# One row of a late load is split off by columns and dealt out by partitions 0 to 125 and 126 to 127

## The chip, the cores and the metric

The kernel runs on one core of one Trainium2 chip. The metric is device time in microseconds (us), and lower is better. Times of whole runs come as a median of several runs; the profile is one profiled execution of the same program.

## The reference

```python
def setup_inputs():
    batch, seq, dim = 32, 512, 1024
    return {"x": np.random.randn(batch, seq, dim).astype(np.float32)}

def reference(x):
    relu_x = np.maximum(x, 0)
    return np.sum(relu_x, axis=-1).astype(np.float32)
```

The input has 32 x 512 = 16,384 rows of 1,024 float32 numbers, 67.1 MB. Of each row the negative numbers are set to zero and the rest is summed, so the output is 16,384 numbers, 64 KB.

## The kernel before

The 16,384 rows lie on 128 partitions, so each partition has 128 rows, and these come as 8 blocks of 16 rows. A block is 64 KB per partition and 8.4 MB in all. Three buffers (`io`) in the on-chip memory take the blocks in turn. All loads and stores are issued by SP (SyncE) on one queue and share the core's 16 DMA engines. The order of the work is written out by hand: every load has a semaphore of its own, and a load that reuses a buffer waits on the count `sems.dve` that says that VectorE (DVE) has done with it.

- **Blocks 0 to 6** (the loop over `NB` in `relu_sum`): ScalarE (ACT) clamps the block in place in pieces (`clamp`, L145), VectorE sums each piece (`total`, L153). Of block 6 ACT takes two rows with sum (`act_row`, L160) and block 6's last eight rows go to VectorE, which clamps and sums a row in one instruction (`dve_row`, L168, 14 such rows up to the end).
- **The last 16 rows** come in smaller loads, so that the work behind the last byte is short. `TAIL = [8, 4]` gives a load of 8 rows and a load of 4 rows per partition; in each, rows are shared between ACT and VectorE one by one. The last four rows come as four loads that are cut by columns of the partition's 4,096 numbers: 2,302 columns, then the last 873 columns, then 518, and at the very end 403 columns into a tile named `last`. ACT, VectorE and GpSimd (POOL, L246) clamp and sum the parts (`act_part` L122, `dve_part` L127); one instruction of VectorE (L266) joins the parts of the last row but one.
- **The stores** (`store`, L115 and L116): the sums of block 0, the sums of nearly all other rows, and at the very end the sums of the last two rows.

TensorE multiplies a few tiles from the buffers beside the tail (L186); nothing reads its result.

The load of 4 rows per partition is one DMA of 128 partitions x 4,096 numbers (16,384 bytes per partition, 2 MB). Its first row is ACT's and its second VectorE's, each of which waits for 16 counts on the load's semaphore; then ACT and VectorE take one more row each. "The twelfth of the last 16 rows" is the last row of this load. Behind it in the queue stand the loads of 2,302, 873, 518 and 403 columns.

Of the kernel before, what the change touches and what calls it, by code (L numbers as in the profile page):

```python
# [10 lines left out]
NBUF = 3  # L11
# [15 lines left out]

EARLY = 1
N_MM, MM_COLS = 8, 512


def kernel(tc: tile.TileContext, x: bass.AP, out: bass.AP):
    nc = tc.nc
    sems = Semaphores(tc)

    tc.close()
    tc.compile()
    nc.cur_bb = nc.bb_map[tc.start_bb_name]
    body = nc.cur_bb.bb.instructions
    ends = list(body)  # L40
    body.clear()
    n_stores = relu_sum(nc, sems, x, out)
    body.extend(ends)


    nc.cur_bb = nc.bb_map[tc.start_bb_name + "_end"]
    nc.cur_bb.bb.instructions.clear()
    nums = sorted(s.num for s in (*sems.loads, sems.act, sems.dve))
    cleared = range(nums[0], nums[-1] + 1)
    assert len(cleared) == len(nums)  # L50
    nc.sync.sem_clear(cleared)
    nc.sync.wait_ge(sems.stored, 16 * n_stores).then_inc(sems.stored, -16 * n_stores)
    open_without_barrier(tc, EARLY)
# [12 lines left out]
def relu_sum(nc, sems: Semaphores, x: bass.AP, out: bass.AP):  # L66
    x_flat = x.flatten_outer_dims()
    N, D = x_flat.shape
    NT = N // P
    NB = len(TWO)  # L70
# [5 lines left out]
    res = nc.alloc_sbuf_tensor("res", [P, NT], F32)  # L76
# [13 lines left out]
    def rows(m, n):  # L90
        if m < ROWS:
            return xf[:, m : m + n, :]
        return xv[:, m - ROWS : m - ROWS + n, :]
# [6 lines left out]
    n_load = n_act = n_dve = n_store = 0  # L100

    def load(dst, src, after=None):
        nonlocal n_load
        dma = nc.sync.dma_start(out=dst, in_=src)  # L104
        if after:
            dma.wait_op(sems.dve, after[1], "sem-ge")
        dma.then_inc(sems.loads[n_load], 16)
        n_load += 1
        return sems.loads[n_load - 1]

# [44 lines left out]
        ).wait_op(sems.act, n_act, "sem-ge").then_inc(sems.dve, 1)  # L155
        n_dve += 1

    def act_row(ap, accum_out, loaded):
        nonlocal n_act
        i = nc.scalar.activation(out=ap, in_=ap, func=RELU, accum_out=accum_out)  # L160
        if loaded is not None:
            i.wait_op(loaded, 16, "sem-ge")
        i.then_inc(sems.act, 1)
        n_act += 1

    def dve_row(ap, accum_out, loaded):
        nonlocal n_dve
        i = nc.vector.tensor_scalar(  # L168
            out=ap,
            in0=ap,  # L170
            scalar1=0.0,
            scalar2=None,
            op0=MAX,
            op1=ADD,
            accum_out=accum_out,
        )
        if loaded is not None:
            i.wait_op(loaded, 16, "sem-ge")
        i.then_inc(sems.dve, 1)
        n_dve += 1  # L180

# [10 lines left out]
    freed = []  # L192
    m = 0
    for j in range(NB):
        buf = bufs[j % NBUF]
        loaded = load(buf[:, :, :], rows(m, ROWS), j >= NBUF and freed[j - NBUF])
        c = 0
        act_waits = dve_waits = loaded
        for n in TWO[j]:
            clamp(buf[:, c : c + n, :], act_waits)  # L200
            total(buf[:, c : c + n, :], m + c, n)
            act_waits = None
            c += n
        for _ in range(ACT[j]):
            act_row(buf[:, c, :], res[:, m + c : m + c + 1], act_waits)
            act_waits = None
            c += 1
        for _ in range(DVE[j]):
            dve_row(buf[:, c, :], res[:, m + c : m + c + 1], dve_waits)
            dve_waits = None  # L210
            c += 1
        assert c == ROWS
        freed.append((n_act, n_dve))
        m += ROWS
# [2 lines left out]
    multiply(freed[-1][1])  # L217
    buf = bufs[NB % NBUF]
    c = 0
    for n in TAIL:  # L220
        loaded = load(
            buf[:, c : c + n, :], rows(m, n), None if c else freed[NB - NBUF]
        )
        for i in range(n):
            if i % 2 == 0 or (n == 8 and i == 7):
                act_row(buf[:, c, :], res[:, m : m + 1], loaded if i == 0 else None)
            else:
                dve_row(buf[:, c, :], res[:, m : m + 1], loaded if i == 1 else None)
            c += 1
            m += 1  # L230

    flat = buf[:, :, :].rearrange("p c d -> p (c d)")
    src = rows(m, 4).rearrange("p c d -> p (c d)")
    at = c * D
    head = 2 * D + HEAD
# [2 lines left out]


    loaded = load(flat[:, at : at + head], src[:, :head])  # L240
    act_row(buf[:, c, :], res[:, m : m + 1], loaded)
    sums_act = n_act
    dve_row(buf[:, c + 1, :], res[:, m + 1 : m + 2], loaded)
    sums_dve = n_dve
    clamped = flat[:, at + 2 * D : at + head]
    nc.gpsimd.tensor_scalar(  # L246
        out=clamped, in0=clamped, scalar1=0.0, scalar2=None, op0=MAX
    ).wait_op(loaded, 16, "sem-ge").then_inc(sems.end, 1)
    for lo, hi, n, first, second in (
# [3 lines left out]
        loaded = load(flat[:, at + lo : at + hi], src[:, lo:hi])  # L253
        act_part(flat[:, at + lo : at + lo + n], last[:, first : first + 1], (loaded, 16))
        dve_part(flat[:, at + lo + n : at + hi], last[:, second : second + 1], (loaded, 16))
    loaded = load(last[:, 2 : 2 + n_last], src[:, middle:end])
# [10 lines left out]
        out=clamped,  # L267
# [5 lines left out]
        accum_out=res[:, NT - 2 : NT - 1],  # L273
# [53 lines left out]
```

## Time and profile before

| | us |
|---|---|
| three runs | 160.9, 161.08, 161.12 |
| median of the runs | 161.08 |
| span of the profiled execution | 159.9 |
| between span and median of the runs | 1.18 |
| the 16 DMA engines' packets, share of the span | 97.8% |
| VectorE busy | 118.7 (74%) |
| ScalarE busy | 103.6 (65%) |
| last load has landed, start of the last sum (L266) | 158.05 |

The span runs from the first issue on SP to the landing of the last store, and is the profiled execution's own time; the time of a run has 1.0 to 1.2 us more around it. All DMA packets of the input, 67.1 MB, are in one queue. The 16 DMA engines can be told apart by the order of their packets: each load gives each engine eight packets, one for each of its eight partitions' rows, and then one increment of the load's semaphore; the work that waits for a load starts at the sixteenth increment.

### The profile page before, as it was taken

The numbers are of one execution on the slowest core, as the hardware profiler recorded it, in microseconds if no ns is written. First come the engines' busy times: TensorE is split into PE (matmuls) and PEld (weight loads), VectorE is DVE, ScalarE is ACT, GpSimd is POOL, SyncE is SP. The second block draws the span as 40 slices with busy tenths as digits, with TensorE's granted clock in tenths as the row PEclk, the third lists the DMA queues.
The fourth block names the chain that finished last, engine by engine and source line by source line (L and its number), as shares of the span: only waits on it lengthen the run. The fifth ranks groups of instructions, "written<-read, shape, count | busy, mean of one in ns | idle before, by whom it ended". The sixth has DMA issues, their size and how long they took to land.

```text
span 159.9 us, 157 instructions
## 1 busy us (share of the span) xinstructions
PE 8.6 (5%) x16; PEld 3.6 (2%) x16; DVE 118.7 (74%) x44; ACT 103.6 (65%) x53; POOL 1.0 (1%) x5
## 2 busy tenths in 40 slices
PE   0000000000000000000000000000000000000695
PEld 0000000000000000000000000000000000000241
DVE  0000000006999799999999999999999799999986
ACT  0000049993599807997099950999429993397995
POOL 0000000000000000000000000000000000000001
DMA  8996996996996997999979979969969969899993
GB/s 279 508 492 295 524 492 295 524 492 295 525 492 295 524 475 311 524 393 393 525 328 459 508 344 459 508 295 508 492 295 524 492 295 524 377 402 402 428 396 110
DMA packets 2304, 67.18 MB, mean 420 GB/s; under 512 B 640, under 2 KB 768, under 8 KB 1024
## 3 DMA queue, kind: packets, MB, share of 16 engines
q1 hardware_dynamic: 2304, 67.18, 97.8%
HBM read 67.11 MB, written 0.07 MB: 420 GB/s over the span
## 4 chain that ended last, share of the span: by engine, by line
DMA 45%; DVE 45%; ACT 9%; SPq 1%; issue 0%
DMA io<-in_x_dram 45%; DVE res L153 43%; ACT io L145 9%; DVE io L168 1%; SPq L104 1%; DVE io L127 1%; DVE io L266 0%
## 5 line engine op out<-in xcount | busy, mean ns | idle before, releaser
L153 DVE TENSOR_REDUCE res<-io 128x8 f32<-128x8192 f32 (+2 forms) x10 | 101.1, 10173 | 39.2 <-ACT io L145 39.2
L145 ACT ACTIVATE io<-io 128x8192 f32<-128x8192 f32 (+2 forms) x10 | 81.8, 8218 | 25.9 <-DMA io<-in_x_dram 25.9
L160 ACT ACTIVATE io<-io 128x1024 f32<-128x1024 f32 x18 | 18.8, 1042 | 6.6 <-DMA io<-in_x_dram 6.6
L186 PE MATMUL ps<-io 128*128 128x512 f32 x16 | 8.6, 698 | 149.5 <-DVE io L168 149.5
L168 DVE TENSOR_SCALAR_CACHE_REDUCE io<-io 128x1024 f32<-128x1024 f32 x14 | 16.2, 1215 | 0.5 <-DMA io<-in_x_dram 0.4
L143 ACT ACT_TABLE_LOAD x1 | 1.3, 1283 | 22.3 <-DMA io<-in_x_dram 22.3
L186 PEld LDWEIGHTS ps<-io 128*128 128x128 f32 x16 | 3.6, 231 | 153.7 <-DVE io L168 149.5
L160 ACT ACTIVATION_READ_ACCUMULATOR io<-io 128x1 f32 x18 | 3.3, 186 | 0.0
L246 POOL TENSOR_SCALAR io<-io 128x254 f32<-128x254 f32 x1 | 0.8, 841 | 155.4 <-DMA io<-in_x_dram 155.4
L168 DVE DVE_READ_ACCUMULATOR io<-io 128x1 f32 x14 | 1.2, 82 | 0.0
L127 DVE TENSOR_SCALAR_CACHE_REDUCE io<-io 128x552 f32<-128x552 f32 (+1 forms) x2 | 1.1, 594 | 0.0
L122 ACT ACTIVATE io<-io 128x321 f32<-128x321 f32 (+1 forms) x2 | 0.9, 426 | 0.1
L266 DVE SCALAR_TENSOR_TENSOR io<-last,io 128x254 f32<-128x254 f32 x1 | 0.4, 423 | 0.0
L122 ACT ACTIVATION_READ_ACCUMULATOR io<-io 128x1 f32 x2 | 0.4, 186 | 0.0
L122 ACT ACTIVATE last<-last 128x153 f32<-128x153 f32 x1 | 0.3, 330 | 0.0
L122 ACT ACTIVATION_READ_ACCUMULATOR last<-last 128x1 f32 x1 | 0.2, 187 | 0.0
L127 DVE DVE_READ_ACCUMULATOR io<-io 128x1 f32 x2 | 0.2, 82 | 0.0
L311 POOL MEMSET const-uint8-127<- 128x1 uint8 x1 | 0.1, 102 | 0.0
L311 POOL MEMSET const-bfloat16-1.0<- 128x1 bf16 x1 | 0.1, 101 | 0.0
L311 POOL MEMSET const-float32-0.0<- 128x1 f32 x1 | 0.1, 99 | 0.2 <-issue 0.2
L311 POOL MEMSET const-float32-1.0<- 128x1 f32 x1 | 0.1, 98 | 0.0
L266 DVE DVE_READ_ACCUMULATOR io<-last,io 128x1 f32 x1 | 0.1, 82 | 0.0
## 6 DMA issues: line engine op xcount, KB each, us to landing
io<-in_x_dram SPq DMA_DIRECT2D x1, 4096.0 KB, 23.7
io<-in_x_dram SPq DMA_DIRECT2D x1, 2048.0 KB, 28.3
io<-in_x_dram SPq DMA_DIRECT2D x1, 1151.0 KB, 30.6
io<-in_x_dram SPq DMA_DIRECT2D x1, 436.5 KB, 31.2
io<-in_x_dram SPq DMA_DIRECT2D x1, 259.0 KB, 31.4
last<-in_x_dram SPq DMA_DIRECT2D x1, 201.5 KB, 31.4
io<-in_x_dram SPq DMA_DIRECT2D x7, 29.0
out_dram<-res SPq DMA_DIRECT2D x1, 55.0 KB, 1.6
```

The costliest lines, as they stand in the source:

```text
L104: dma = nc.sync.dma_start(out=dst, in_=src)
L122: nc.scalar.activation(out=ap, in_=ap, func=RELU, accum_out=accum_out).wait_op(*after, "sem-ge").then_inc(sems.end, 1)
L127: i = nc.vector.tensor_scalar(out=ap, in0=ap, scalar1=0.0, scalar2=None, op0=MAX, op1=ADD, accum_out=accum_out,)
L143: nc.scalar.preload_act_table(RELU).wait_op(loaded, 16, "sem-ge")
L145: i = nc.scalar.activation(out=ap, in_=ap, func=RELU)
L153: nc.vector.tensor_reduce(out=res[:, m : m + n], in_=ap, axis=mybir.AxisListType.X, op=ADD).wait_op(sems.act, n_act, "sem-ge").then_inc(se ...
L160: i = nc.scalar.activation(out=ap, in_=ap, func=RELU, accum_out=accum_out)
L168: i = nc.vector.tensor_scalar(out=ap, in0=ap, scalar1=0.0, scalar2=None, op0=MAX, op1=ADD, accum_out=accum_out,)
L186: i = nc.tensor.matmul(ps[:, :], rows_of[:, 0, :P], rows_of[:, 1, :MM_COLS], start=True, stop=True)
L246: nc.gpsimd.tensor_scalar(out=clamped, in0=clamped, scalar1=0.0, scalar2=None, op0=MAX).wait_op(loaded, 16, "sem-ge").then_inc(sems.end, 1)
L266: nc.vector.scalar_tensor_tensor(out=clamped, in0=last[:, : 2 + LAST_DVE], scalar=0.0, in1=clamped, op0=MAX, op1=ADD, accum_out=res[:, NT ...
L311: nc = _bacc.Bacc("TRN2", target_bir_lowering=False, num_devices=1)
```

## The change

Of the load of 4 rows per partition, the last 334 columns (of 4,096, so 1,336 bytes of the 16,384) are left out and come in two loads of their own right behind it: one for partitions 0 to 125, one for partitions 126 and 127. All three increase the same semaphore, and the two instructions that waited for 16 counts on it now wait for 48. SP issues two DMAs more; nothing else is moved. The functions `act_row` and `dve_row` get the count as an argument, 16 by default.

```diff
+MOST, SHARED = 126, 334
...
     def load(dst, src, after=None):
+        return load_parts([(dst, src)], after)
+
+    def load_parts(parts, after=None):
         nonlocal n_load
-        dma = nc.sync.dma_start(out=dst, in_=src)
-        if after:
-            dma.wait_op(sems.dve, after[1], "sem-ge")
-        dma.then_inc(sems.loads[n_load], 16)
+        for dst, src in parts:
+            dma = nc.sync.dma_start(out=dst, in_=src)
+            if after:
+                dma.wait_op(sems.dve, after[1], "sem-ge")
+            dma.then_inc(sems.loads[n_load], 16)
+            after = None
         n_load += 1
         return sems.loads[n_load - 1]
...
+    flat = buf[:, :, :].rearrange("p c d -> p (c d)")
     for n in TAIL:
-        loaded = load(
-            buf[:, c : c + n, :], rows(m, n), None if c else freed[NB - NBUF]
-        )
+        count = 16
+        if c == 0:
+            loaded = load(buf[:, c : c + n, :], rows(m, n), freed[NB - NBUF])
+        else:
+            count = 16 * 3
+            src = rows(m, n).rearrange("p c d -> p (c d)")
+            at, cut = c * D, n * D - SHARED
+            loaded = load_parts(
+                [
+                    (flat[:, at : at + cut], src[:, :cut]),
+                    (flat[:MOST, at + cut : at + n * D], src[:MOST, cut:]),
+                    (flat[MOST:, at + cut : at + n * D], src[MOST:, cut:]),
+                ]
+            )
         for i in range(n):
             if i % 2 == 0 or (n == 8 and i == 7):
-                act_row(buf[:, c, :], res[:, m : m + 1], loaded if i == 0 else None)
+                act_row(buf[:, c, :], res[:, m : m + 1], loaded if i == 0 else None, count)
             else:
-                dve_row(buf[:, c, :], res[:, m : m + 1], loaded if i == 1 else None)
+                dve_row(buf[:, c, :], res[:, m : m + 1], loaded if i == 1 else None, count)
```

## The prediction

> **What bounds the kernel now.** I read the shares of busy time first, then the DMA queue, then the chain of waits.
>
> ```profile
> PE 8.6 (5%) x16; PEld 3.6 (2%) x16; DVE 118.7 (74%) x44; ACT 103.6 (65%) x53; POOL 1.0 (1%) x5
> ...
> q1 hardware_dynamic: 2304, 67.18, 97.8%
> ```
>
> The reader is to see that the packets of the DMA queue take 97.8% of what 16 DMA engines have, while VectorE has a quarter of the span free. The chain in order of time says the same of the end:
>
> ```profile
> 125.15 30.57 DMA io<-in_x_dram
> 155.72 0.02 issue
> 155.75 1.23 DVE io L168 x2
> 156.97 1.05 DVE io L127 x4
> 158.03 0.02 issue
> 158.05 0.43 DVE io L266 x2
> ```
>
> A load issued at 125.15 us lands at 155.72 us, and that is no slow transfer: it stands in the queue behind the loads before it. From then on VectorE has 2.26 us of work in a row (up to 158.01), and the last load lands at 158.03. So two things end within 0.02 us of each other: the work behind the load of 2,302 columns, and the last load itself. To make the end earlier, both loads must land earlier.
>
> Which of the 16 DMA engines lands last? Stretches of 0.1 us near the end show it; the last two numbers of a row are the mean busy share of the 16 engines and GB/s.
>
> ```profile
> core 0: us, PE busy (x) PEld busy (x) DVE busy (x) ACT busy (x) POOL busy (x), PEclk, DMA share, GB/s
> 156.40:156.50 0.10, 0.10 (x1) 0.01 (x1) 0.10 (x1) 0.10 (x1) 0.10 (x1) 1.00 1.09 394
> ...
> 156.80:156.90 0.10, 0.10 (x2) 0.04 (x1) 0.10 (x3) 0.10 (x3) 0.00 (x0) 1.00 0.74 243
> ...
> 157.00:157.10 0.10, 0.10 (x2) 0.02 (x1) 0.10 (x1) 0.10 (x1) 0.00 (x0) 1.00 0.28 60
> ...
> 157.20:157.30 0.10, 0.10 (x2) 0.07 (x1) 0.10 (x1) 0.10 (x2) 0.00 (x0) 1.00 0.09 32
> ...
> 157.40:157.50 0.10, 0.10 (x1) 0.00 (x0) 0.10 (x1) 0.04 (x1) 0.00 (x0) 1.00 0.10 21
> ```
>
> All engines work until 156.5; from 157.1 to 157.5 the share is 0.1 to 0.2, about two engines of 16. The increments of the load semaphores tell the same, load by load (us, for 14 engines and then the two late ones): four rows 151.97 to 152.43, then 152.82 and 152.93; 2,302 columns up to 155.22, then 155.61 and 155.72; 403 columns up to 157.56, then 157.91 and 158.03. Two engines are late by 0.35 to 0.50 us each time. They are not slower: a 64 KB packet takes 2.42 us on every engine, 27.1 GB/s. They are late from the start: the first packets of the 16 engines begin from 1.01 to 1.84 us, the two that begin last (1.61 and 1.84) end their first packet at 4.98 and 4.85, the others by 4.50. Since every engine gets the same bytes and never runs dry, the lag stays to the end.
>
> **The change, part by part.**
>
> 1. *The price of a packet.* The medians of the packet records are 68 ns for 1,612 bytes and 611 ns for 16,384. The line through both is 8.7 ns and 36.8 ns per 1,000 bytes. It gives 562 ns for the new 15,048 bytes and 58 ns for 1,336. Packets start 3 to 4 ns before the former one's record ends, so 54 to 58 ns is the range; I take 58.
>
> 2. *The 334 columns leave the main load.* Each engine's eight packets shrink by 49 ns each: 8 x 49 = 0.39 us less, on every engine.
>
> 3. *The load of 126 partitions.* The trace has no load on fewer than 128 partitions, so its dealing has to be bounded. In the trace 128 rows go as 8 to each of 16 engines, always evenly. 126 rows go evenly to 14 engines, 9 each, and neither to 15 nor to 16. The ends are 16 engines (7 or 8 rows each, nothing gained) and one engine (126 x 58 = 7.3 us); I take 14, as nearest to the even dealing seen. The cost is 9 x 58 = 0.52 us on each of the 14 engines, and none on the two left out. The Trainium skill, "DMA: Bandwidth & Descriptors", section "Why a DMA increments its semaphore by 16 and not by 1", says that the count of engines is the largest up to 16 that divides the slowest dimension, and that the lowest-numbered engines are taken; by that 14 are used too, but nothing here shows it.
>
> 4. *Which two are left out.* If rows are dealt in order, the two without rows are those that are served last, and the two late engines are those whose first packet began last. I take these for the same.
>
> 5. *The load of partitions 126 and 127.* Two rows of 58 ns, one on each of two engines, or both on one: 0.06 to 0.12 us there. If the first engines get them, these are ahead of the late ones by about half a microsecond.
>
> 6. *Two more issues on SP.* Issues at L104 took 327 to 486 ns, median 407, so the four loads behind and the first store are issued 0.8 us later. Cover: the last load's issue moves from 126.65 to 127.5, and its first bytes are due near 157; SP then waited 29.3 us (L115). Without that cover the cost would be the 0.8 us. I put it at nothing.
>
> 7. *The wait for 48 counts* stands at two instructions that waited for this load anyway. Behind ACT's and VectorE's row queue all later rows of their engine, and the last store waits for them. Before, VectorE waited until 152.95; it was free at 152.87. It costs nothing if the parts land earlier.
>
> **The sum.** The two late engines: 0.39 us earlier. The other fourteen: 0.52 - 0.39 = 0.13 us later (0.10 to 0.19, the last for one with a tenth row). At the load of 2,302 columns the late ones come to 155.33 and the others to 155.35: earlier by 0.37. At the last load the late ones come to 157.64 and the others to 157.56 + 0.13 = 157.69: earlier by 0.34. The engines follow: ACT is free at 155.34 and VectorE at 155.2, and VectorE's 2.26 us from 155.38 on end at 157.64. So the end moves by **0.34 us** (0.28 to 0.38), the profiled span from 159.9 to 159.56. Around the span the median run has 1.18 us, which I leave alone: **160.74 us**, own range 160.70 to 160.80. A measurement of this kernel can tell about 0.2% (0.32 us) from no change; the forecast lies barely beyond it.
>
> **Rivals.**
>
> *The destination is shared, so nothing is gained (161.0 to 161.08).* A packet's rate of 27.2 GB/s may be the limit of where it writes rather than of the engine. Now each engine writes the same eight partitions in every load; nine rows in a load of 14 engines must fall on partitions that other engines fill. If the late engines' partitions take in 27.2 GB/s at most, the 8 x 49 ns taken from a late engine return as waiting for the helpers' rows: 0.39 - 0.39 = 0, and the end stays but for gaps of 9 ns per packet (some 10 packets, 0.1 us). For it: all 16 engines run at one rate. Against it: an engine's own limit would look the same. The Trainium skill, "SBUF — State Buffer", section "Door 1: The DMA port swizzle", says that 16 ports to the partitions bound DMA at 27.2 GB/s each, which is this rule and speaks against the change; the 27.1 GB/s of the 64 KB packets agrees with the figure, not with where the limit sits.
>
> *The helpers get stuck (161.26 to 161.78).* The same crossing, but with time lost: if each of the 9 rows takes twice 58 ns, the fourteen end 9 x 116 - 392 = 0.65 us later, 0.18 behind the old end; if engines also lose as much on their own rows, 0.70. It decides from 96 ns a row (9 x 96 - 392 = 471, today's lead), and passes 0.2% at 132. For it: the first packets took up to 3.38 us in place of 2.42, so packets can be held up. Against it: from then on hardly one was.
>
> *Fewer engines than 14 (over 161.1).* With eight engines or fewer, 16 rows x 58 - 392 = 0.54 us exceeds the lead of 0.47. With two engines: 63 x 58 - 392 - 471 = 2.8 us, 163.9.
>
> *The wrong engines are spared (161.0 to 161.2).* If one of the late two stays among the fourteen, it lands 0.13 us later; the end moves by +0.01 to +0.13 us.
>
> **How the numbers follow.** The forecast has 0.57: 0.47 beyond 0.2%, 0.10 below it, since its bounds cross that line. The shared destination has 0.16 (0.13 within 0.2%, 0.03 slower), the wrong engines 0.08 (within), stuck helpers 0.15 and fewer engines 0.04 (both slower). That makes 0.47 faster, 0.31 same, 0.22 slower. The range runs from 160.55 (the largest gain, 0.38 us, and 0.15 us of scatter like that of the three runs) to 161.3, the cheaper end of the stuck helpers; it leaves out some 0.15.
>
> **What would show it.** In the profile after: at the four-row load and behind it the sixteen increments lie closer together, without two that are 0.35 us late; the share of 0.1 to 0.2 before the last landing is gone or shorter. There are 126 packets of 1,336 bytes on 14 engines, of 54 to 60 ns; far longer ones speak for the crossing. The load of 2,302 columns lands near 155.35 and the last near 157.69. I am wrong if two engines are late by half a microsecond as before, or if the packets of 1,336 bytes, or those of the late engines beside them, are stretched.

## The result and the profile after

The changed kernel takes 161.46 us (median of 20 runs, 161.23 to 161.91) against 161.1 us before (20 runs, 160.88 to 161.33). The ratio is 1.0023, 95% interval 1.0017 to 1.003: 0.36 us slower, where 0.34 us faster was forecast. The profiled execution took 161.29 us and has a span of 160.0 us. That is only 0.1 us more than the span of the trace before: the trace after is of one of the faster executions, and in the trace before the last engine happened to lag the most (see the mis-sized term below). So the loss is read here from the steps inside the traces, and its size from the medians.

The page, engines and DMA queue:

```profile
PE 8.7 (5%) x16; PEld 3.6 (2%) x16; DVE 118.8 (74%) x44; ACT 103.5 (65%) x53; POOL 1.0 (1%) x5
...
q1 hardware_dynamic: 2448, 67.18, 98.1%
```

The same bytes come in 144 packets more (128 of them rows of 1,336 bytes, 16 of them increments), and the engines' packets fill 98.1% of the span in place of 97.8%. The end of the chain in order of time:

```profile
125.72 29.97 DMA io<-in_x_dram
155.69 0.02 issue
155.72 1.23 DVE io L174 x2
156.94 1.09 DVE io L133 x4
158.04 0.02 issue
158.06 0.43 DVE io L283 x2
```

It is the chain of before within 0.03 us: the load of 2,302 columns lands at 155.69 (155.35 was forecast), the last one at 157.99 (157.69). The stretches of 0.1 us near the end show that this is not because nothing happened. The last two numbers are again the busy share and GB/s.

```profile
core 0: us, PE busy (x) PEld busy (x) DVE busy (x) ACT busy (x) POOL busy (x), PEclk, DMA share, GB/s
156.40:156.50 0.10, 0.10 (x1) 0.00 (x0) 0.10 (x1) 0.10 (x1) 0.10 (x1) 1.00 1.13 435
...
156.80:156.90 0.10, 0.10 (x1) 0.00 (x0) 0.10 (x3) 0.10 (x2) 0.00 (x0) 1.00 1.13 421
...
157.00:157.10 0.10, 0.10 (x2) 0.07 (x1) 0.10 (x1) 0.10 (x1) 0.00 (x0) 1.00 1.18 435
...
157.20:157.30 0.10, 0.10 (x1) 0.02 (x1) 0.10 (x1) 0.10 (x2) 0.00 (x0) 1.00 0.85 218
...
157.40:157.50 0.10, 0.10 (x2) 0.00 (x0) 0.10 (x1) 0.00 (x0) 0.00 (x0) 1.00 0.26 46
```

From 157.0 to 157.3 nearly all engines work now, where the share before was 0.28 and then 0.09, about four engines and then one or two. The sixteen increments of the last load (each engine's signal that its part has landed) lie within 0.36 us (157.64 to 157.99) where they had 0.93 (157.10 to 158.03). So the engines were evened out, but the early ones were brought back by half a microsecond and the late ones not brought forward. Where it was lost, stretches of 2 us show. Before:

```profile
151.00:153.00 2.00, 2.00 (x4) 0.84 (x3) 1.92 (x5) 2.00 (x5) 0.00 (x0) 1.00 0.99 417
153.00:155.00 2.00, 2.00 (x6) 0.82 (x5) 2.00 (x3) 2.00 (x5) 0.00 (x0) 1.00 0.96 396
```

After:

```profile
151.00:153.00 2.00, 2.00 (x4) 0.87 (x3) 1.69 (x4) 2.00 (x5) 0.00 (x0) 1.00 0.96 311
153.00:155.00 2.00, 2.00 (x6) 0.88 (x5) 2.00 (x3) 2.00 (x5) 0.00 (x0) 1.00 0.99 411
```

Between 151 and 153 us, when the rows of 1,336 bytes go, the engines are about as busy as before (0.96, before 0.99) and move 311 GB/s in place of 417: their packets got longer. The packet records say which. Most rows of 1,336 bytes take the 58 ns of the forecast, but the later ones up to 100; the eight packets of 9,208 bytes behind them have a median of 353 ns, yet the first of them takes 476 to 556 on every engine and the second up to 528, where none took more than 355 before.

For the experiments I use two numbers of a trace besides the time: from the increments of the load of 8 rows to those of the last load, the mean of the sixteen engines and the step from last to last. Before: mean 10.00, last 9.99 us. After: 10.45 and 10.16. The engines lost 0.45 us on average in that stage.

### The profile page after: what moved, and what is told of

Its sections match the earlier page's. It is cut to its first block, busy times and chain, and to the rows that moved or that the text cites. A ratio compares the mean times of both kernels' runs of the same rounds, so it can differ in the third digit from the quotient of the medians.

```text
span 160.0 us, 159 instructions
## 1 busy us (share of the span) xinstructions
PE 8.7 (5%) x16; PEld 3.6 (2%) x16; DVE 118.8 (74%) x44; ACT 103.5 (65%) x53; POOL 1.0 (1%) x5
## 3 DMA queue, kind: packets, MB, share of 16 engines
q1 hardware_dynamic: 2448, 67.18, 98.1%
## 4 chain that ended last, share of the span: by engine, by line
DVE 45%; DMA 44%; ACT 9%; SPq 1%; issue 0%
DMA io<-in_x_dram 44%; DVE res L159 43%; ACT io L151 9%; SPq L109 1%; DVE io L174 1%; DVE io L133 1%; DVE io L283 0%
```

## The experiments

Theories: **crossing** (rows that land on partitions which another engine fills in every other load lose time), against **packets** (more and smaller packets, issues, increments), **source** (rows read from memory that another engine reads) and **uneven deal** (14 engines carry more). Ratios are to runs of the kernel before on the same chip, with the 95% interval; all were timed in five rounds. "Mean" and "last" are of the one profiled execution of each kernel, and such an execution can lie up to 0.39 us from its kernel's median (e6 162.26 against 161.87, e5 161.60 against 161.28, e7 161.38 against 161.68), so differences of a few hundredths there are not secured.

| kernel | ratio | mean, us | last, us |
|---|---|---|---|
| before | 1 | 10.00 | 9.99 |
| the change | 1.0023 (1.0017 to 1.003) | 10.45 | 10.16 |
| e1_plain128 | 1.0009 (1.0001 to 1.0018) | 10.08 | 10.08 |
| e2_112_16 | 1.0028 (1.0017 to 1.004) | 10.43 | 10.40 |
| e3_source | 1.0004 (0.9996 to 1.0013) | 10.08 | 10.08 |
| e4_half | 1.0011 (1.0003 to 1.002) | 10.34 | 10.18 |
| e5_last | 1.0018 (1.0009 to 1.0027) | 10.36 | 10.38 |
| e6_double | 1.0056 (1.0043 to 1.007) | 11.00 | 11.15 |
| e7_halves | 1.0039 (1.0026 to 1.0051) | 10.42 | 10.43 |
| e8_tiny | 1.0003 (0.9993 to 1.0013) | 10.04 | 10.05 |
| e9_not_late | 1.0029 (1.0018 to 1.004) | 10.51 | 10.36 |
| e10_late_only | 1.0001 (0.9992 to 1.001) | 9.93 | 10.02 |
| e11_none | 0.9974 (0.9965 to 0.9983) | 9.63 | 9.64 |
| e12_elsewhere | 0.999 (0.9981 to 0.9998) | 9.91 | 9.86 |

In each kernel the counts that the instructions wait for are set to match its loads; the diffs below leave that out.

### e1_plain128: the columns in a load of their own, nothing crosses

```diff
-                    (flat[:MOST, at + cut : at + n * D], src[:MOST, cut:]),
-                    (flat[MOST:, at + cut : at + n * D], src[MOST:, cut:]),
+                    (flat[:, at + cut : at + n * D], src[:, cut:]),
```

> The 334 columns come in one load of their own for all 128 partitions, so each engine keeps its own eight rows. Crossing theory (the loss comes from rows that land on partitions which another engine fills in every other load): no loss but 8 more packets of 9 ns per engine, +0.05 to +0.1 us over before, and the late two engines stay late by 0.35 to 0.5 us. Packet theory (small packets, one more issue and one more increment cost more than I took): the mean landing of the sixteen engines moves by most of the 0.45 us that the changed kernel shows, and the time by +0.3.

Measured: mean +0.07 us, time +0.14 us by medians (a little above the stated +0.05 to +0.1). All rows of 1,336 bytes took 58 or 59 ns and no packet of 9,208 bytes more than 366. Packets are 0.07 of the 0.45 us.

### e2_112_16: all cross, nobody is spared

```diff
-MOST, SHARED = 126, 334
+MOST, SHARED = 112, 334
```

> The 334 columns come as partitions 0 to 111 and 112 to 127: 7 rows and 1 row for each of 16 engines, so no engine is spared and all carry the same bytes, but nearly all rows lie on partitions of another engine. Crossing theory: stretched packets of 1,336 bytes and of 9,208 bytes behind them, the mean landing 0.3 to 0.6 us later, time +0.3 to +0.8 us over before. Uneven-deal theory (the loss is that fourteen engines carry nine or ten rows): +0.05 to +0.15 us. Packet theory: like the load of 128 partitions.

Measured: mean +0.43 us, time +0.35 by medians; rows of 1,336 bytes up to 107 ns, packets of 9,208 up to 562. The same 128 rows in one load more cost 0.35 us more in the mean than in e1, because they are dealt differently (the one load and its increments more are no cause, see e8). Here every engine carries eight rows, so the unequal number of rows is not what costs. In the same stretch, first e1 and then e2:

```profile
151.00:153.00 2.00, 2.00 (x4) 0.82 (x3) 1.84 (x5) 2.00 (x5) 0.00 (x0) 1.00 0.94 379
```

```profile
151.00:153.00 2.00, 2.00 (x4) 0.82 (x3) 1.63 (x4) 2.00 (x5) 0.00 (x0) 1.00 0.97 321
```

Both send the same small rows (so both are below 417), but dealt as 112 + 16 partitions 58 GB/s fewer get through at a share that is no lower.

### e3_source: crossing on the reading side alone

```diff
+    N2 = N1 - 9 * (NT - ROWS)
+    xo = x_flat[N2 : N2 + P * (NT - ROWS)].rearrange("(p m) d -> p m d", p=P)
...
-                    (flat[:, at + cut : at + n * D], src[:, cut:]),
+                    (flat[:, at + cut : at + n * D], other[:, cut:]),
```

> As the load of 334 columns for 128 partitions, but its rows are read from nine partitions further up in the input (the sums of these 128 rows are of other data): each engine writes its own partitions and reads rows that other engines read else. Crossing at the destination: like the plain load of 128 partitions, +0.05 to +0.1 us. Source theory (the loss comes from reading rows of memory that another engine reads): stretched packets and +0.3 us or more.

Measured: as e1 (mean +0.08 us, no row over 59 ns). Reading rows from nine partitions further up costs nothing here beyond the packets; the source theory is out.

### e4_half, e8_tiny and e6_double: 168, 32 and 668 columns

```diff
-MOST, SHARED = 126, 334
+MOST, SHARED = 126, 168
```

> The change with 168 columns in place of 334. Crossing theory: the loss goes with the bytes that cross, about half, +0.1 to +0.25 us over before, the mean landing +0.2 to +0.3 us. A fixed cost of the loads on 14 and 2 engines: +0.3 to +0.4 us as with 334. Spared engines gain 0.19 us on the main load in any case.

> The change with 32 columns, 128 bytes per row. If there is a fixed loss per crossing load (a wait at its increments or at the passage to the next load): the mean landing still moves by 0.2 us or more, time +0.15 us or more. If the loss goes with the bytes: mean +0.1 us (packets alone), time within 0.1 us of before.

> The change with 668 columns in place of 334. From the mean landing of the sixteen engines (from the load of 8 rows to the last load), 0.34 us more than before with 168 columns and 0.45 with 334: if the loss is a fixed part and a part that goes with the bytes, 0.65 to 0.70 with 668, and the time +0.5 to +0.9 us. If it saturates (only the passage from one load to the next is disturbed): mean +0.45 to +0.5, time +0.3 to +0.5 us.

Measured in the mean: +0.04 us with 32 columns, +0.34 with 168, +0.45 with 334, +1.00 with 668; in the time by medians +0.08, +0.16, +0.36, +0.94. There is no fixed price of a load on 14 or 2 engines: e8 has them all and cannot be told from before. The loss grows with the bytes per row, though not in a straight line. No size gains. Two stated sizes were missed: with 168 columns the mean should have lost 0.2 to 0.3 us, and with 668 the loss of mean and time lies above both ranges that were stated. With 668 columns the packets of 9,208 bytes reach 705 ns.

### e5_last: the very last load is dealt, with nothing behind it

```diff
-    loaded = load(last[:, 2 : 2 + n_last], src[:, middle:end])
+    loaded = load_parts(
+        [
+            (last[:MOST, 2 : 2 + n_last], src[:MOST, middle:end]),
+            (last[MOST:, 2 : 2 + n_last], src[MOST:, middle:end]),
+        ]
+    )
```

> The four-row load is whole again; instead the very last load (403 columns) is dealt as partitions 0 to 125 and 126 and 127, with nothing behind it. Engine theory (a late engine is bound by its own packets, and the loss comes only from what stands behind the crossing rows): the late engine is spared 8 x 68 = 0.54 us, the others carry one packet of 68 ns more, and the end moves earlier by the lag of that execution, 0.2 to 0.4 us. Shared-destination theory (a partition's bytes take the same time whoever brings them): no gain beyond 0.1 us, the last rows on the late engines' partitions are the last to land; time from -0.1 to +0.3 us.

Measured: 161.28 against 160.93 us, +0.35 by medians; so the loss is not only in what stands behind the rows. The end of the chain:

```profile
125.94 31.89 DMA io<-in_x_dram
157.83 0.02 issue
157.85 0.49 DVE io L133 x2
158.34 0.02 issue
158.37 0.43 DVE io L279 x2
```

VectorE now waits for the load of 518 columns, the one ahead of the dealt one: it lands at 157.83, 2.29 us behind the load of 2,302 columns (155.54), where before it took 1.79 (155.72 to 157.51). Its packets of 2,072 bytes go up to 149 ns (96 before). Packets alone are not the half microsecond: the last one of 2,072 bytes ends at 156.95 (157.05 before), and the last increment of that load follows 0.88 us later in place of 0.46. So while the helpers bring their rows, an engine that still works on the load in front is held up by 0.5 us, about the 0.54 that the late engine was spared; the greater part of it is seen only between the packet and its increment.

### e7_halves: two loads of 64 partitions

```diff
-MOST, SHARED = 126, 334
+MOST, SHARED = 64, 334
```

> The 334 columns come as partitions 0 to 63 and 64 to 127, four rows for each of 16 engines in each. Shared-destination theory with a destination that serves 8 partitions at the rate of one engine: if the half of 64 partitions reaches half of the destinations, two engines share one and each row costs up to twice 58 ns, so the mean landing moves by 0.09 + up to 0.46 us, time +0.3 to +0.6 us. Without such sharing: +0.14 us as with the plain load of 128 partitions.

Measured: mean +0.42 us, time +0.75 by medians, above the stated 0.3 to 0.6. It loses what the theory allows, but e2, which does not keep to one half, loses the same in the mean; so it does not single out the halves.

### e9 to e12: which partitions the rows land on

These load only some rows of the 334 columns. The first list is e10's, the second e12's; e9 has (0, 88) and (96, 120), e11 none.

```diff
-                    (flat[:MOST, at + cut : at + n * D], src[:MOST, cut:]),
-                    (flat[MOST:, at + cut : at + n * D], src[MOST:, cut:]),
+                    (flat[88:96, at + cut : at + n * D], src[88:96, cut:]),
+                    (flat[120:128, at + cut : at + n * D], src[120:128, cut:]),
...
+                    (flat[64:72, at + cut : at + n * D], src[64:72, cut:]),
+                    (flat[96:104, at + cut : at + n * D], src[96:104, cut:]),
```

> None of the 334 columns is loaded (their part of the sums is of old data). All engines are spared 0.39 us and nothing crosses: time -0.3 to -0.4 us against before, on either theory. It is the scale for the other two.

> The complement: of the 334 columns only partitions 88 to 95 and 120 to 127 are loaded, eight rows for each of two loads on eight engines; the other 112 rows are left out. Every engine's main packets are 0.39 us shorter in sum. Shared-destination theory: the two last engines wait for these sixteen rows, about 8 x 49 = 0.39 us each, and land as late as before; time -0.1 to +0.1 us. Engine theory: they keep what they are spared, time -0.25 to -0.4 us, as where none of the 334 columns is loaded.

> As the kernel with partitions 88 to 95 and 120 to 127, with the same loads on the same eight engines, but partitions 64 to 71 and 96 to 103. Shared-destination theory: two engines other than the late ones are held up by 0.39 us and come back to where they were, the late ones keep what they are spared; time -0.2 to -0.4 us. If any sixteen crossing rows disturb all engines alike, this kernel takes the same time as the one with partitions 88 to 95 and 120 to 127.

> Of the 334 columns only partitions 0 to 87 and 96 to 119 are loaded, on 11 and 12 engines; 16 partitions are left out, those that would belong to the two last engines if partitions are dealt as 0-3 and 32-35 to the first engine and so on. If a row delays only the engine that fills its partitions: the two last engines' eighth packet of 15,048 bytes stays at 562 to 570 ns (711 and 594 with the change), while the others are still stretched in the load behind; time +0.0 to +0.4 us. If crossing rows disturb all engines alike: the late engines' packets are stretched as with the change.

Measured: without the 334 columns the time falls by 0.45 us by medians (0.3 to 0.4 was stated). (TensorE's last multiplication then ends at 159.23, as late as the span of 159.2, so the scale may be short by 0.1.) With sixteen rows on partitions 88 to 95 and 120 to 127 the whole gain is gone: 160.97 against 160.99. Those sixteen rows take 58 ns each, 0.93 us of one engine's time; yet the mean of all sixteen engines is 0.30 us later than in e11, 4.8 us in sum; the two loads and their increments account for about 0.04 us of the 0.30, by e8. The stretches of e10 and then of e11:

```profile
151.00:153.00 2.00, 2.00 (x4) 0.87 (x3) 1.86 (x5) 2.00 (x5) 0.00 (x0) 1.00 0.92 339
```

```profile
151.00:153.00 2.00, 2.00 (x4) 0.97 (x3) 2.00 (x5) 2.00 (x5) 0.00 (x0) 1.00 0.91 383
```

A 44 GB/s drop at one busy share, though e10 moves more bytes in all. Engines that carry none of the sixteen rows have packets of 9,208 bytes of 474 and 446 ns, or 356 and 588, between 151.4 and 152.4.

e12 moves the sixteen rows to other partitions and is a half miss: the mean loses nearly as much (0.28 us), while the time comes to 0.999, between e11 and e10. So most of the loss is general, and the further part that depends on which partitions the rows land on is about 0.1 to 0.2 us (last to last 9.86 against 10.02); the intervals of e10 and e12 overlap, so that part is not secured. The engine whose main part ends last leans the same way: in e10 its eighth main packet takes 689 ns and the next of 9,208 bytes 558, in e12 633 and 460 (562 and 347 undisturbed). No run shows which partitions an engine fills; that 88 to 95 and 120 to 127 are those of the late engines is the assumption under which e9, e10 and e12 were built. e9 is a miss for the strict form of the theory: with no row on partitions 88 to 95 and 120 to 127 a packet of 15,048 bytes still took 733 ns (711 with the change), and the time, +0.52 us by medians, lies above the stated +0.0 to +0.4. If the assumption holds, a row delays more than the engine that fills its partitions.

## Why the prediction was wrong, point by point

*What bounds the kernel* was right. Both loads named still set the end, and their landing decides (155.69 and 157.99, then 158.06).

*Parts 1 and 2 (prices of packets)*: right where nothing crosses. Main packets take 562 ns, rows 58.

*Part 3 (14 engines)*: right. In the trace after, 34 increments come for the four-row load: two at 125.52 and 125.85, before any data, and 32 later, 16 + 14 + 2. In e9, with 11 and 12 engines, there are 41, which is 2 + 16 + 11 + 12. The Trainium skill's rule on the count of engines ("DMA: Bandwidth & Descriptors", "Why a DMA increments its semaphore by 16 and not by 1") agrees with these.

*Part 4 (the late engines are spared)*: right in this trace. The two engines whose main part ends last, at 151.69 and 152.04, go straight on to a packet of 9,208 bytes, and they are the two that came last at the load of 8 rows.

*Parts 6 and 7 (issues, the wait for 48)*: right. The two more issues, at 124.93 and 125.43, put off the issue of the load behind them by 0.8 us (counted from the issue of the load of 8 rows), and that load lands at its old time; e8, with the same issues and the same wait, is the same as before.

*The sum* is the step that failed. It put 58 ns on a row wherever it lands, nothing on the packets beside and behind these rows, and it let the late engine keep its 0.39 us. None of this held:

- The fourteen: forecast +0.13 us. The mean engine lost 0.45: 0.07 for packets (e1), the other 0.38 through the way the rows are dealt. Little of it lies in the rows themselves: 36 of the 128 took more than 60 ns, 0.06 us per engine beyond 58 ns each. The packets of 9,208 bytes behind them took 0.31 us per engine more than before.
- The late ones: forecast -0.39 us. In the trace after, the last engine's eighth main packet took 711 ns in place of 562 and its first two of 9,208 bytes 495 and 432 in place of 347. That is 149 + 148 + 85 = 382 ns, or 0.38 of the 0.39 us given back. From its 4-byte packet (the increment) behind the load of 8 rows to that behind the load of 2,302 columns it needs 7.64 us, where the last engine needed 7.63 before. The last to finish that load is now an engine that carries rows of 1,336 bytes.

So it was the rival of the stuck helpers joined to that of the shared destination, both priced separately. Of the former the price was near (+0.18 to +0.70 us; measured +0.36), but its place was not: it reckoned from the rows on the helpers, and the time was lost mostly in the packets of all engines behind them. The prediction's own sign of being wrong, stretched packets of the late engines beside the rows, is what came. The Trainium skill, "SBUF — State Buffer", "Door 1: The DMA port swizzle", by which each of the 16 ports to the partitions takes in 27.2 GB/s, would explain the late engines' share of it; e12 against e10 leans that way, and e9 speaks against its being all. The same skill, "DMA: Bandwidth & Descriptors", section "Back-pressure in remote DMA", says of writes between cores that a saturated destination clogs the path back to the sources and to engines that share it. The stretched packets of engines without such a row (e10) look like this; the path itself no run here shows. So it is shown that the dealing of the rows costs the time, and that neither more packets, nor the source, nor an unequal number of rows does; why the packets of the other engines get longer is argued, not shown.

*A second term was mis-sized, and would have mattered had the rest been right.* The lag to be won was taken from one execution, at 0.49 us between the last and the fourteenth engine (at the load of 8 rows). All fourteen kernels are the same up to there, and their profiled executions give 0.05 to 0.49, median 0.28; the trace of before was the largest of them. With 0.28 us, even engines that keep what they are spared gain 0.28 - 0.13 = 0.15 us at the end, less than half the forecast and within what a measurement can tell.

The range (160.55 to 161.3) ended at the cheaper end of the stuck helpers; the result lies 0.16 us beyond.

## What to carry to other kernels

Before work is moved from a late DMA engine to the others, ask where the bytes land: here a load on all 128 partitions cost no more than its packets (e1), and with 672 bytes per row and more every other cut that was tried (126 + 2, 112 + 16, 64 + 64) lost time. Read the size of a lag from several executions before cutting to fit it. If the busy share of the DMA engines stays while GB/s fall, look for longer packets, not for missing ones.

## What the hardware showed unexpectedly

- Sixteen rows of 1,336 bytes in two loads of eight partitions (e10), themselves at 58 ns each, delayed the sixteen engines by 0.30 us on average, also engines that carried none; 128 such rows as 112 + 16 partitions (e2 against e1) delayed them by 0.35. The number of rows counts for little, the bytes per row for more: as 126 + 2 partitions, 128 bytes next to nothing (0.04 us), 2,672 bytes 1.00 us.
- The same rows read from nine partitions further up (e3) cost nothing beyond their packets; dealt to the engines in another way than a load of 128 partitions, they do.
- A landing can be held up behind the packet: in e5 the last increment of the load of 518 columns comes 0.88 us after the load's last packet has ended, before 0.46.
- The lag of the last engine, set by the first packets, differs from execution to execution, from 0.05 to 0.49 us, and stays nearly constant from the first load to the 8-row load (in the trace of before the last engine is 0.50 us behind the fourteenth at the first load and 0.49 at the load of 8 rows).
